# Four GLA heads through one 16-step value product, with merge gates and keys computed beside the GLA levels and kept in DRAM

## The chip, the core and the metric

The kernel runs on one core of one Trainium2 chip. The metric is device time in microseconds of one execution; the time of a kernel is the median of several runs. TensorE (PE) multiplies, VectorE (DVE) and ScalarE (ACT) do the element-wise work, GpSimd (POOL) some of it, and SyncE (SP) issues most DMAs. Each engine works through its own queue in order.

## The reference, cut to what matters

One transformer layer for 256 latent tokens `x` and 256 context tokens `ctx`, width 2048, float32. It has two token mixers side by side (windowed attention A, gated linear attention B), per-channel merge gates, an output projection, and a convolutional FFN.

```python
mod_x = split(silu(c) @ w_mod + b_mod, 6)          # shift, scale, gate twice
qa, ka, va, qb, kb, vb, rb, gf, gb, gate_a, gate_b = project_heads(modulate(x, ...), w_in)
# the same projections of ctx; of them ka, va, kb, vb and the decays are used
o_attn = windowed_attention(qa, ka, va, cka, cva, sink)
sf, sb, _ = context_gla(...)                       # end states of the context
o_gla = latent_gla(qb, kb, vb, gf, gb, sf, sb)     # 4 heads, key width 256, value width 512
y_att = o_attn @ w_attn_o
y_gla = (rms_norm(o_gla, gla_norm) * silu(rb)) @ w_gla_o
x = x + mod_x[2] * ((sigmoid(gate_a) * y_att + sigmoid(gate_b) * y_gla) @ w_out)
x = x + mod_x[5] * conv_ffn(modulate(x, g_ffn, mod_x[3], mod_x[4]), w_up, conv_w, conv_b, w_down)
```

For each GLA head the kernel forms a matrix A (latent rows by latent and context columns, decays included), so that the head's output is A · V with V = h · W_V, h the modulated tokens. By associativity that is also (A · h) · W_V, "the matrix times activations first".

## The kernel before

**Weights.** A float32 product is made of three matmuls on halves. Each 256 x 512 piece of a weight is loaded by SP into a tile `raw` (512 KB; pool `wr`, 7 buffers), rounded by ACT into `whi` (L220), and DVE subtracts to get `wlo` (L221); `whi` and `wlo` have 3 buffers each (`wsplit_raw`). Activations are kept as hi and lo halves too.

**Blocks and ticks.** A block is 512 columns of a weight, contracted in 8 ticks of 256 rows: `proj_nat` (tokens on the output's partitions) and `proj_T` (weight columns on them). With latent and context tokens (`h_xc`, four output tiles, or `h_both`) a tick has 24 matmuls, with latent tokens alone (`h_x`, two tiles) 12. When the block ends, `evac` copies the accumulators out of PSUM. `tick()` and `midway()`, called in each tick, run what was put off to later ticks (`defer`), the next GLA level (`beside`, at a rate per tick), and background steps (`bg_steps` at `bg_rate`): `mod_latent` computes the modulation rows that are needed later from `w_modT`, 96 steps here, each a 512 KB load and one multiply-and-sum on DVE (L403).

**Order.** A scheduler with priorities arranges the instructions on each engine (splits of weights have high priority, and buffers limit how far ahead they can stand); `in_order` pins pairs.

**Stages, in order.** (1) Start, up to 195 us: modulation, the first columns of queries, keys and values of all tokens, group by group; the value columns are head 0's `VB` block, kept in `vb0`. (2) Heads 0 to 3 of GLA, 195 to 435 us: `with_gla(h, kb, block)` runs `gla_A`, the levels that build A of head h, beside a block of projections: `kb_block` (head 0), `v_block` of head 1's values (head 1), `VA` (head 2) and `KA` (head 3), the last two kept in SBUF tiles `va32`, `ka32` (L1060). Heads 0 and 1 multiply A with their values in `gla_o`. (3) The `GA` block for j = 0, and `pair_values` for heads 2 and 3, 435 to 541 us: 8 steps of an `inner` product, 24 matmuls into `pg` (A times 256 columns of h), and an `outer` one, 24 into `acc` (times the weight of two heads). `natural(kp)` normalizes and modulates the 256 columns of x and ctx for a step (L1146, L1152, on DVE and POOL). (4) Attention, 541 to 745. (5) `rb_block`, then the merge: for each j of 0 to 3, 8 ticks each of `GA` (j > 0; L1372 evacuates it), `w_attn_o`, `GB` (L1383 evacuates it, as sigmoid) and `w_gla_o`, up to 1130 us, with the background steps at rate 0.75. (6) `w_out` and the FFN, to the end.

## Time and profile before

| | |
|---|---|
| median of 3 runs | 1946.02 us (1945.85 to 1946.04) |
| the profiled execution | 1945.88 us, its span 1944.1 us |
| PE busy | 1928.8 us (99%), 9906 instructions |
| DVE busy | 1436.2 us (74%) |
| ACT busy | 992.2 us (51%) |
| POOL busy | 58.1 us (3%) |
| DMA | 429.26 MB, 221 GB/s in the mean |
| PE's clock | 1.00 in most windows, 0.999 in the mean |

The span runs from the first to the last instruction. A row of a window lists busy time and instruction counts by engine in this order: PE, PEld (weight load), DVE, ACT, POOL, then PE's granted clock, the share of the DMA engines in use and their rate. In rows of groups, `out<-in xcount | busy, mean ns of one | idle time ahead of it`. In rows of the timeline, the start and the duration come first.

### The profile page before, as it was taken

What the parts mean: (1) busy time and instruction counts of PE and PEld (TensorE: products, weight loads), DVE (VectorE), ACT (ScalarE), POOL (GpSimd) and SP (SyncE); (2) the same over time, 40 slices, a digit from 0 to 9 for tenths busy, and PEclk for the clock granted to TensorE, in tenths of its full rate; (3) what the DMA queues carried; (4) which work ended last, traced back from release to release, by engine and by line L of the source; (5) the groups of instructions that cost most, each with busy time, mean ns of one, the idle gap of its engine ahead of it and who ended that gap; (6) DMA issues with size and microseconds to landing.
All of it is one profiled execution on the core that took longest, in us unless ns stands there. A gap on an engine that the chain in (4) does not pass through costs nothing.

```text
span 1944.1 us, 26485 instructions
## 1 busy us (share of the span) xinstructions
PE 1928.8 (99%) x9906; PEld 1603.9 (83%) x9906; DVE 1436.2 (74%) x2217; ACT 992.2 (51%) x1443; POOL 58.1 (3%) x72
## 2 busy tenths in 40 slices
PE   8999999999999999999999999999999999999999
PEld 6678888888887788888888888888888888888887
DVE  5656867687967889987888577998886545777654
ACT  5223666654456655444444445755565334655532
POOL 0010011020100000000000000000000000000000
PEclk9999999999999999999999999999999999999999
DMA  9984222226554456999999877688886666666663
GB/s 395 412 303 145 67 78 73 78 85 216 179 163 120 141 169 213 350 334 321 334 336 334 300 263 236 200 274 283 274 279 215 193 192 191 187 190 190 195 214 111
DMA packets 188208, 429.26 MB, mean 221 GB/s; under 512 B 12960, under 2 KB 17312, under 8 KB 182832
## 3 DMA queue, kind: packets, MB, share of 16 engines
q1 hardware_dynamic: 186416, 421.84, 65.6%
q0 software_dynamic: 1488, 5.57, 0.9%
q8 instruction: 77, 1.26, 0.3%
q14 instruction: 51, 0.42, 0.1%
q10 hardware_dynamic: 176, 0.17, 0.0%
HBM read 425.37 MB, written 2.16 MB: 220 GB/s over the span
## 4 chain that ended last, share of the span: by engine, by line
PE 96%; DMA 3%; DVE 0%; ACT 0%; issue 0%; SPq 0%
PE acc L84 73%; PE accs L84 13%; PE pa L96 2%; PE pg L84 2%; PE poa L96 1%; PE pS L96 1%; DMA mraw<-in_w_mod 1%; PE pm L96 1%; DMA xr<-in_ctxT 1%; PE ptp L99 1%; DMA raw<-in_w_in 1%; PE po L96 1%; PE pto L99 0%; DMA pack<-in_k_pack 0%; PE plr L646 0%; PE pz L96 0%
## 5 line engine op out<-in xcount | busy, mean ns | idle before, releaser
L220 ACT ACTIVATE whi<-raw 128x1024 fp32r<-128x1024 f32 x568 | 601.2, 1060 | 716.6 <-PE acc L84 541.0
L221 DVE TENSOR_TENSOR wlo<-raw,whi 128x1024 fp32r<-128x1024 f32 x568 | 695.1, 1226 | 348.4 <-ACT whi L220 339.3
L84 PE MATMUL accs<-h,whi 128*128 128x512 f32 x704 | 244.5, 392 | 0.0
L84 PE MATMUL acc<-h,whi 128*128 128x512 f32 x640 | 222.3, 392 | 0.0
L84 PE MATMUL accs<-h,wlo 128*128 128x256 f32 x704 | 196.0, 278 | 0.0
L84 PE MATMUL acc<-h,wlo 128*128 128x256 f32 x640 | 178.1, 278 | 0.0
L84 PEld LDWEIGHTS accs<-h,whi 128*128 128x128 f32 x704 | 131.8, 187 | 29.9
L84 PEld LDWEIGHTS acc<-h,whi 128*128 128x128 f32 x640 | 119.8, 187 | 27.0
L84 PE MATMUL acc<-whi,ah 128*128 128x512 f32 x352 | 137.0, 389 | 0.0
L84 PE MATMUL acc<-whi,al 128*128 128x512 f32 x352 | 137.0, 389 | 0.0
L84 PEld LDWEIGHTS accs<-h,wlo 128*128 128x128 f32 x704 | 132.5, 188 | 0.0
L84 PEld LDWEIGHTS acc<-h,wlo 128*128 128x128 f32 x640 | 120.5, 188 | 0.1
L84 PE MATMUL acc<-whi,h2hi 128*128 128x512 f32 x256 | 101.3, 396 | 0.0
L84 PE MATMUL acc<-whi,th 128*128 128x512 f32 x256 | 100.5, 393 | 0.0
L84 PE MATMUL acc<-whi,h3hi 128*128 128x512 f32 x256 | 100.4, 392 | 0.0
L84 PE MATMUL acc<-whi,h2lo 128*128 128x512 f32 x256 | 99.8, 390 | 0.0
L84 PE MATMUL acc<-whi,h3lo 128*128 128x512 f32 x256 | 99.8, 390 | 0.0
L84 PE MATMUL acc<-whi,tl 128*128 128x512 f32 x256 | 99.7, 389 | 0.0
L84 PE MATMUL acc<-wlo,ah 128*128 128x512 f32 x352 | 94.3, 389 | 0.0
L84 PE MATMUL acc<-whi,h1hi 128*128 128x512 f32 x224 | 88.3, 394 | 0.0
L84 PE MATMUL acc<-whi,h0hi 128*128 128x512 f32 x224 | 87.8, 392 | 0.0
L84 PE MATMUL acc<-whi,h1lo 128*128 128x512 f32 x224 | 87.6, 391 | 0.0
(416 smaller groups left out, 3549.3 us busy)
## 6 DMA issues: line engine op xcount, KB each, us to landing
raw<-in_w_in SPq DMA_DIRECT2D x204, 512.0 KB, 4.3
raw<-in_w_up SPq DMA_DIRECT2D x176, 512.0 KB, 4.4
raw<-in_w_modT SPq DMA_DIRECT2D x128, 512.0 KB, 5.2
raw<-in_w_down SPq DMA_DIRECT2D x88, 512.0 KB, 4.0
mraw<-in_w_mod SPq DMA_DIRECT2D x32, 1024.0 KB, 14.0
raw<-in_w_attn_o SPq DMA_DIRECT2D x32, 512.0 KB, 5.6
raw<-in_w_gla_o SPq DMA_DIRECT2D x32, 512.0 KB, 5.6
raw<-in_w_out SPq DMA_DIRECT2D x32, 512.0 KB, 5.3
```

Of the source, the lines that this page charges most:

```text
L84: r = pe_seq(PE.matmul(*a, **k))
L96: return pe_seq(after(PE.matmul(*a, **k)))
L99: return pe_seq(after(PE.transpose(*a)))
L220: j = S.activation(hi[:, 0:n, :], raw[:, 0:n, :], AF.Copy).ins
L221: i = V.tensor_tensor(lo[:, 0:n, :], raw[:, 0:n, :], hi[:, 0:n, :].bitcast(F32), op=ALU.subtract).ins
```

## The change

1. In stage 1 the values of attention (`VA`, tile `va0`) take the place of head 0's `VB` block; POOL stores them to DRAM (`dva`).
2. All four heads' matrices are kept (`pair_x`, `pair_c`, two pairs); `gla_o` and `v_block` are gone, and `all_values` runs 16 steps of inner and outer products, 8 for each pair.
3. Head 1 has the `KA` block beside it, stored to DRAM (`dka`). Heads 2 and 3 have the four `GA` and the four `GB` blocks beside them (12 matmuls per tick, levels at rate 0.3 per tick). `kept` evacuates two tiles into one buffer of the weight pool and POOL stores it (`da0` to `db3`).
4. Background steps run beside heads 2 and 3 at rate 0.45, and in rb and merge at 0.85. With `share=True`, all of them in the first place and every second one in the other is a multiply on POOL (L415), a sum by ACT (L392) and an addition of one column on DVE. `natural` uses no POOL, and its rows come for two steps at a time.
5. The merge has `w_attn_o` and `w_gla_o` only; POOL fetches the gates from DRAM (`kept_gate`), ACT takes their sigmoid. Keys and values of attention are loaded back from `dka` and `dva` by SP.

The core of the diff:

```diff
-    def mod_latent(parts, begin=None):
+    def mod_latent(parts, begin=None, share=False):
...
+        def drain():
+            while sums:
+                d, c, base = sums.pop(0)
+                in_order(last_lo[0], V.tensor_tensor(d, c, base, op=ALU.add).ins)
+            while open_:
+                raw, d, base, c = open_.pop(0)
+                in_order(last_hi[0], S.activation(raw, raw, AF.Copy, accum_out=c).ins)
+                sums.append((d, c, base))
...
+            drain()
+            if share and (i % 2 == 0 or beside):
+                G.tensor_tensor(raws[i], raws[i], row[0], op=ALU.mult)
+                open_.append((raws[i], d, base, scale1[:, 0, i % 16:i % 16 + 1]))
+                return
             i0 = V.tensor_tensor_reduce(out=raws[i], in0=raws[i], in1=row[0], scale=1.0,
...
-    proj_nat(w_in, 0, VB, kts, h_x, lambda i, b: S.activation(vb0[:, i, :], b, AF.Copy))
+    proj_nat(w_in, 0, VA, kts, h_x, lambda i, b: S.activation(va0[:, i, :], b, AF.Copy))
...
+    dva = dram.tile([P, 4, 512], F32, name="dva")
+    G.dma_start(dva, va0)
...
-    a, kb1 = with_gla(0, kbt, kb_block, [lambda i=i: first_values(i) for i in range(4)])
-    gla_o(0, a, *v)
-    defer(2, send_rows)
-    a, v = with_gla(1, kbt, lambda: v_block(VB + 512, "v1"))
-    gla_o(1, a, *v)
-
-    def kept(c0, name):
-        t = []
+    def kept(c0, name, lhs, by_tile=False):
+        n = len(lhs)
+        d = dram.tile([P, n, 512], F32, name=name)
+        raw = []
 
         def evac(i, b):
-            if not t:
-                t.append(M(name, [P, 4, 512]))
-            S.activation(t[0][:, i, :], b, AF.Copy)
-
-        proj_nat(w_in, 0, c0, ALL, h_xc, evac, by_tile=True)
-        return t[0]
-
-    va32 = with_gla(2, kb1, lambda: kept(VA, "va32"))[1]
+            if i % 2 == 0:
+                raw[:] = [wr.tile([P, 2, 512], F32, name="raw", tag="raw")]
+            S.activation(raw[0][:, i % 2, :], b, AF.Copy)
+            if i % 2:
+                G.dma_start(d[:, i - 1:i + 1, :], raw[0])
+
+        proj_nat(w_in, 0, c0, ALL, lhs, evac, by_tile=by_tile)
+        return d
...
-    ka32 = with_gla(3, kb1, lambda: kept(KA, "ka32"))[1]
+    defer(2, send_rows)
+    kb1 = with_gla(0, kbt, kb_block)
+    dka = with_gla(1, kbt, lambda: kept(KA, "dka", h_xc, True))
+    gate_a, gate_b = [], []
+
+    def gate_blocks(c0, name, to):
+        for j in range(4):
+            if c0 == GB and j == 3:
+                defer(0, lambda: fetch(0))
+                defer(2, lambda: natural(0))
+                defer(5, lambda: natural(1))
+            to.append(kept(c0 + j * 512, f"{name}{j}", h_x))
...
+    bg_rate[:] = [0.45, 0.0]
+    with_gla(2, kb1, lambda: gate_blocks(GA, "da", gate_a), 0.3)
+    with_gla(3, kb1, lambda: gate_blocks(GB, "db", gate_b), 0.3)
+    bg_rate[:] = [0.0, 0.0]
...
-        for kp in range(n + 1):
-            if kp + 1 < n and kp:
-                natural(kp + 1)
-            if kp < n:
-                inner(kp)
-            if kp:
+        for step in range(KT + 1):
+            if 0 < step < KT - 1:
+                natural(step + 1)
+            if step < KT:
+                inner(step)
+            if step:
+                pair, kp = divmod(step - 1, KT // 2)
                 for i in range(2):
                     tick()
...
-    bg_rate[0] = 0.75
+    bg_rate[0] = 0.85
     for j in range(1, 4):
         rb_block(j)
...
+    def kept_gate(d, name):
+        m = [W2("fc", name, [P, 512]) for _ in range(2)]
+        for t in range(2):
+            G.dma_start(m[t], d[:, t, :])
+            i = S.activation(m[t], m[t], AF.Sigmoid)
+            in_order(exps[-1], i.ins)
+            sig.append(i)
+        return m
+
     for j in range(4):
...
+        a1 = kept_gate(gate_a[j], "m1")
+        a2 = kept_gate(gate_b[j], "m2")
...
         proj_nat(A["w_attn_o"][0], 0, j * 512, ALL, [h_tok(1, 0), h_tok(1, 1)], at_evac)
-        proj_nat(w_in, 0, GB + j * 512, ALL, h_x,
-                 lambda t, b, a2=a2: sig.append(S.activation(a2[t], b, AF.Sigmoid)))
```

## The prediction

> **What bounds the kernel now.** I read the page first, then windows by stage, the chain, the waits, and the timeline at block ends.

> ```profile
> span 1944.1 us, 26485 instructions
> PE 1928.8 (99%) x9906; PEld 1603.9 (83%) x9906; DVE 1436.2 (74%) x2217; ACT 992.2 (51%) x1443; POOL 58.1 (3%) x72
> ```

> The profiled execution took 1945.88 us, 0.14 below the median of the three runs (1946.02). TensorE is busy for 99% of it, so only two things can move the time: the number of matmuls, and places at which TensorE would now have to wait. By stage (columns: window, length, busy us of PE, PEld, DVE, ACT, POOL with counts, clock, DMA share, GB/s):

> ```profile
> 0.00:97.00 97.00, 86.69 (x640) 61.03 (x641) 62.68 (x138) 39.63 (x59) 0.84 (x5) 1.00 1.00 404
> 323.50:434.90 111.40, 111.40 (x578) 95.43 (x576) 81.58 (x158) 64.43 (x126) 15.62 (x23) 1.00 0.28 80
> 434.90:541.00 106.10, 106.10 (x477) 87.89 (x476) 85.01 (x126) 46.78 (x66) 13.13 (x9) 1.00 0.61 186
> 745.00:1130.00 385.00, 385.00 (x1734) 318.77 (x1733) 309.35 (x376) 170.50 (x183) 0.00 (x0) 1.00 0.90 317
> 1830.00:1944.10 114.10, 109.53 (x484) 90.35 (x483) 63.70 (x71) 44.03 (x46) 0.00 (x0) 0.99 0.52 167
> ```

> TensorE idles 10.3 us before 97 and 4.6 us after 1830, both outside the change; in the stages that the change rebuilds (323 to 541: heads 2 and 3, the GA block, the paired values; 745 to 1130: rb and merge) it idles for nothing. So no wait can be removed there, only work.

> **What the change removes and adds on TensorE.** Heads 0 and 1 lose their value blocks (192 matmuls of v1; the VB block of head 0 only changes places with VA, whose later block of 192 goes) and two `gla_o` of 24. They gain eight more steps of inner and outer products, 24 + 24 each. 192 + 192 + 48 − 192 − 192 = 48 matmuls fewer. Their price, from the chain:

> ```profile
> 256.32 5.44 PE po L96 x24
> 456.14 10.88 PE pg L84 x48
> 467.02 5.44 PE acc L84 x24
> ```

> 24 take 5.44 us, and the 48 `pg` take 10.88. **Term 1: −10.9 us**, all on the path, since TensorE is the path. The GA and GB blocks only move from the merge to heads 2 and 3, at the same number of matmuls.

> **What stands at a block's end.** TensorE is gapless because the splits of the next block stand ahead of the copies that empty the last one. At the end of a GB block in the merge (ACT, then PE; start, duration):

> ```profile
> 920.55 1.06 ACT L220 ACTIVATE whi<-raw 128x1024 fp32r<-128x1024 f32 x1 [1.66 <-PE acc L84]
> 921.52 1.06 ACT L1383 ACTIVATE m<-acc 128x512 f32<-128x512 f32 x2
> ...
> 920.12 0.39 PE L84 MATMUL acc<-whi,h3lo 128*128 128x512 f32 x1
> 920.35 1.07 PE L84 MATMUL acc<-wlo,h3hi 128*128 128x512 f32 x4
> 921.26 0.39 PE L84 MATMUL acc<-whi,th 128*128 128x512 f32 x1
> ```

> The block's last matmuls end at 921.42 and the next block's first began at 921.26, on a split made beforehand; the two copies followed at 921.52. The order of ACT shows the same, two splits of the next block (`whi_7486`, `whi_7507`) ahead of the copies:

> ```order
> L220 ACTIVATE whi_7486<-raw_7484 128x1024 [waits DMAHW7_49,DVE_49,PE_49]
> L220 ACTIVATE whi_7507<-raw_7505 128x1024 [waits DMAHW1_49,DVE_49,PE_49]
> L1383 ACTIVATE m2_7111<-acc_7295 128x512 [waits PE_49]
> L1383 ACTIVATE m2_7112<-acc_7296 128x512 [waits PE_49]
> L220 ACTIVATE whi_7528<-raw_7526 128x1024 [waits DMAHW3_49,DVE_49,PE_49]
> ```

> After the change, ACT at the end of gate block `da1` in head 2 (`whi_3312` is the first split of `da2`; `raw_3303` holds the two kept tiles; `raw_3219` and `raw_3280` are modulation products of POOL that ACT sums):

> ```order
> L916 ACTIVATE k2_3368<-segs_2619 128x8x32
> L1026 ACTIVATE raw_3303<-acc_3056 128x512 [waits DMASW1_49,PE_49]
> L1026 ACTIVATE raw_3303<-acc_3057 128x512 [waits PE_49]
> L220 ACTIVATE whi_3312<-raw_3310 128x1024 [waits DMAHW6_49,Activation_49]
> L392 ACTIVATE raw_3219,scale1_102<-raw_3219 128x1024 [waits Pool_49]
> L220 ACTIVATE whi_3348<-raw_3346 128x1024 [waits DMAHW0_49,Activation_49]
> ```

> The first split has moved behind both copies, and the copies wait for the block's last matmul: ACT can't prepare the next block, and TensorE has nothing of it to do. The same order stands at eight of the boundaries: from `dka` to `da0`, the three between the GA blocks, `da3` to `db0`, and the three between the GB blocks. At the ninth, `db3` to the value steps, two inner products (24 matmuls each, 10.9 us) stand in between and cover it.

> Price of one, put on the rows above: the second copy starts 0.04 us after the last matmul's shown end (as the split at 920.55 does after 920.12 + 0.39), at 921.46; half of the `x2` row is 0.53, and

> ```profile
> L1383 ACT ACTIVATE m<-acc 128x512 f32<-128x512 f32 x8 | 4.4, 586 | 2.1 <-PE acc L84 2.1
> L220 ACT ACTIVATE whi<-raw 128x1024 fp32r<-128x1024 f32 x568 | 601.2, 1060 | 716.6 <-PE acc L84 541.0
> ```

> with 0.59 it ends at 922.05, the split at 923.11, and TensorE takes it up at about 923.2 where it had been at 921.26: 1.95 us. Least: copy and split alone, 1.65; where k2 exponentials stand ahead too (two of the eight), 2.5. **Term 2: 8 × 1.95 = +15.6 us**, ends 13.2 and 18. The split of wlo (1.23 us) comes while the eight matmuls with whi run (1.8 us), and hides.

> **Stores and the loads behind them.** Each kept pair of tiles sits in a buffer of the weight pool until POOL's store has landed, and the pool's order decides which load waits for it. SP before, in head 3 (L105 carries every load):

> ```order
> L105 DMA raw_3245<-in_w_in 128x2x512 [waits DMAHW5_49,DVE_49,Activation_49]
> L105 DMA raw_3311<-in_w_in 128x2x512 [waits DMAHW6_49,DVE_49]
> L105 DMA raw_3366<-in_w_in 128x2x512 [waits DMAHW7_49,DVE_49,Activation_49]
> L105 DMA raw_3428<-in_w_in 128x2x512 [waits DMAHW0_49,DVE_49,Activation_49]
> L105 DMA raw_3485<-in_w_in 128x2x512 [waits DMAHW1_49,DVE_49,Activation_49]
> ```

> SP after, over gate block `da2` (DMASW4 is the landing of `da1`'s store, `raw_3401` the block's fourth weight piece):

> ```order
> L105 DMA raw_3310<-in_w_in 128x2x512 [waits DMAHW6_49,DMAHW2_49,DVE_49]
> L105 DMA raw_3341<-in_w_modT 128x1024 [waits DMAHW3_49,DVE_49]
> L105 DMA raw_3346<-in_w_in 128x2x512 [waits DMAHW0_49,Activation_49]
> L105 DMA raw_3383<-in_w_in 128x2x512 [waits DMAHW5_49,DMAHW1_49,DVE_49]
> L105 DMA raw_3401<-in_w_in 128x2x512 [waits DMASW4_49,Activation_49]
> L105 DMA raw_3439<-in_w_modT 128x1024 [waits Activation_49]
> L105 DMA raw_3444<-in_w_in 128x2x512 [waits DMAHW6_49,DMAHW4_49,DVE_49]
> ```

> Before, loads waited only for splits; now one waits for a store, with two more loads queued behind it. The nearest rows for the path:

> ```profile
> raw<-in_w_in SPq DMA_DIRECT2D x204, 512.0 KB, 4.3
> att<-in_k_amask POOLq DMA_DIRECT2D x1, 512.0 KB, 4.4
> out<-yd SPq DMA_DIRECT2D x8, 256.0 KB, 4.4
> L1085 POOL DMA_DIRECT2D att<-in_k_amask x1 | 0.5, 536 | 2.6 <-ACT q L921 2.6
> ```

> From the block's end: copies 0.9 us, POOL's issue 0.54 (up to 2.5 more if it stands in a multiply), store 4.4, load 4.3, split 1.06: 11.2 to 13.7 us. The fourth piece is needed three ticks later, 3 × 2.72 = 8.2 us, and the drain of 1.95 and the early first use add some 2: 10.1 to 11. A shortfall of 0 to 2 us, in the five of the eight blocks where the order puts such a load so early. **Term 3: +5 us**, one each; ends 0 and 10.

> **DVE and POOL.** 61 products of the modulation leave DVE (L403) for POOL, ACT sums them (61 × 1.06 more on an engine that is half idle), DVE adds one column. The rows of before show what POOL and DVE do to each other:

> ```profile
> 472.17 1.29 POOL L1152 TENSOR_TENSOR raw<-raw,rows 128x512 f32<-128x512 f32 x1 [7.29 <-DVE raw L1146]
> 472.73 1.80 DVE L221 TENSOR_TENSOR wlo<-raw,whi 128x1024 fp32r<-128x1024 f32 x1 [0.70 <-ACT whi L220]
> 506.91 1.22 DVE L221 TENSOR_TENSOR wlo<-raw,whi 128x1024 fp32r<-128x1024 f32 x1
> 507.14 2.14 POOL L1152 TENSOR_TENSOR raw<-raw,rows 128x512 f32<-128x512 f32 x1 [2.98 <-DVE raw L1146]
> L403 DVE CUSTOM_DVE_ANT_0 raw<-raw,csrow,pack 128x1024 f32<-128x1024 f32 x64 | 81.7, 1279 | 0.0
> L221 DVE TENSOR_TENSOR wlo<-raw,whi 128x1024 fp32r<-128x1024 f32 x568 | 695.1, 1226 | 348.4 <-ACT whi L220 339.3
> ```

> Where they meet, the second one grows by what is left of the first: 472.17 + 1.29 = 473.46, and DVE ends 1.07 after that; 506.91 + 1.22 = 508.13, POOL 1.15 after. They take turns. So a 128x1024 multiply on POOL, twice 1.2 or about 2.45 us by this estimate, is time lost to DVE, where the same product took 1.28 on DVE itself: the move adds load. By budgets: heads 2 and 3 now last 64 ticks × 2.72 = 174.2 plus their own products 24.3 (the 111.4 of the window less 384 matmuls at 0.2268), 198.5 us, 214 with term 2. DVE and POOL together need 64 × 1.2 = 77, the levels about 60 (81.6 in that window, less 15 splits at 1.23 and some small ones), 10 for the two `natural` steps, 27 × 2.45 = 66, and 5 for gates: 218. In rb and merge 88 ticks make 248 us, against 88 × 1.2 + 35 × 1.28 + 34 × 2.45 + 19 = 253; some 20 of it, which read PSUM, may run beside POOL. Both stand at the edge. Where the pair falls behind, wlo is late and TensorE waits; the store of the gates stands behind POOL's multiplies. **Term 4: +4 us**, ends 0 and 25, the low end taken since the rates spread the steps evenly and PSUM work overlaps.

> [...]

> **DMA in the merge.** The merge streamed these bytes:

> ```profile
> 954.00:1042.00 88.00, 88.00 (x394) 72.85 (x393) 72.52 (x90) 37.16 (x39) 0.00 (x0) 1.00 0.95 330
> 49.00:97.00 48.00, 47.20 (x318) 30.39 (x318) 33.32 (x73) 12.87 (x18) 0.00 (x0) 1.00 1.02 413
> ```

> After, a tick of 2.72 us loads 1 + 0.85 pieces of 0.524 MB, 356 GB/s, plus gate reads of 4.2 MB over 248 us, 17: 373 GB/s, under the 413 that the early stage reached. I add nothing, and keep it as a rival. The other additions hide: a step of the values is 10.9 us of matmuls against two splits and a `natural`, 2 × 1.23 + 4 × 0.61 + 2 × 0.69 + 1.23 = 7.5 us on DVE, and some 1 for the halves of `pg`, by these rows:

> ```profile
> L1146 DVE SCALAR_TENSOR_TENSOR raw<-raw,pack,rows 128x256 f32<-128x256 f32 x32 | 18.3, 606 | 0.0
> L1152 DVE TENSOR_TENSOR raw<-raw,rows 128x512 f32<-128x512 f32 x8 | 5.5, 692 | 0.2
> ```

> `dka`, `dva` come back 512 KB at a time ahead of their use; the 16 sigmoids (0.6 us each) stand on ACT at 37 of 88 us.

> [...]

> **Sum.** 1945.9 − 10.9 + 15.6 + 5 + 4 = 1959.6, and with 0.1 to the median 1959.7: 1960 us, 0.7% slower.

> **Rivals.**
> Drains at their least and nothing else: 1946.0 − 10.9 + 13.2 = 1948.3, to about 1949.9; for it, POOL and DVE at the edge but not over, and stores that land before their successor is needed; against it, five loads whose path is longer than their lead.
> The other side, faster: a boundary costs under 10.9 / 8 = 1.36 us, if the first copy runs early (tile 0 is done 0.45 us before tile 1) and level products of head 2 or 3 fill TensorE at the boundary. At 0.8 us each it would be 1946 − 10.9 + 6.4 = 1941.5. Against it: the second copy and the split alone are 1.65 us, and these products wait for exponentials on the same ACT.
> The port: POOL and DVE fall behind in both stages. At 2.6 us a multiply instead of 2.45 and no overlap with PSUM work, 6 + 14 us instead of term 4, about 1975.
> The merge by DMA: in 954 to 1042 a share of 0.95 moved 330 GB/s, so the engines would be full at 347 there; 373 is 7% above that, up to 18 us of 248. Half of it, since rb's ticks and the 413 of the early stage say that the limit lies between: +9 in place of term 4's part, 1964 to 1974.

> **How the numbers follow.** Drains with late loads 0.55 (1950 to 1968); drains at their least 0.12; faster 0.04; the port 0.19 (1968 to 1985); DMA 0.10. The range 1948 to 1977 leaves out the faster case and the upper part of the port's. A measurement of this kernel can tell about 0.2%, 3.9 us, from no change: under 1942.1 is 0.04, to 1949.9 0.13, above 0.83.

> **What would show it.** Eight idle stretches of TensorE near 1.95 us at L1026 block ends, released by ACT whi L220; waits of the fourth weight piece of a gate block; POOL at L415 of 2.4 us or more and wlo far above 1.23 beside it; the merge without idle time. Wrong if TensorE runs through the boundaries, or if wlo rather than whi is what it waits for.

## The result, and the profile after

The changed kernel takes 2052.93 us (median of 4 runs, 2049.63 to 2056.86) against 1946.03: a ratio of 1.055 (95% interval 1.0531 to 1.0568), 107 us slower. The prediction said 1960, with a range to 1977. Of the four runs of e3 below, one took 3225.33 us at a granted clock of 0.556, and all figures of e3 are those of the other three.

Page of the changed kernel (its profiled execution took 2056.86 us):

```profile
span 2055.1 us, 26710 instructions
PE 1957.2 (95%) x9858; PEld 1612.2 (78%) x9858; DVE 1507.6 (73%) x2228; ACT 1066.8 (52%) x1591; POOL 222.5 (11%) x152
...
L221 DVE TENSOR_TENSOR wlo<-raw,whi 128x1024 fp32r<-128x1024 f32 x568 | 713.9, 1262 | 385.2 <-ACT whi L220 379.6
...
L415 POOL TENSOR_TENSOR raw<-raw,csrow 128x1024 f32<-128x1024 f32 x61 | 166.7, 2735 | 466.5 <-DVE qT L63 216.0
```

Two subtractions on the second line give the account. TensorE idles for 2055.1 − 1957.2 = 97.9 us, where it idled for 15.3: **82.6 us of waits**. It is busy for 28.4 us longer although it has 48 matmuls (10.9 us) less: **39.3 us of slower matmuls**. 82.6 + 39.3 − 10.9 = 111.0, the difference of the spans. The clock agrees: it was 0.979 in the mean of this execution, which is 43 us of 2055.1, part of it while TensorE stood still. The windows say where (columns as before: PE, PEld, DVE, ACT, POOL, clock, DMA share, GB/s):

```profile
200.00:313.00 113.00, 111.77 (x577) 94.35 (x574) 86.61 (x169) 73.26 (x148) 15.21 (x18) 1.00 0.23 69
313.00:542.00 229.00, 190.84 (x842) 154.27 (x840) 177.94 (x216) 128.70 (x214) 77.62 (x41) 0.90 0.61 206
542.00:600.00 58.00, 46.53 (x188) 38.07 (x189) 30.35 (x40) 22.22 (x28) 14.45 (x17) 0.83 0.66 220
600.00:920.00 320.00, 317.25 (x1446) 257.81 (x1444) 245.52 (x468) 166.50 (x279) 2.96 (x2) 1.00 0.52 160
920.00:1000.00 80.00, 73.07 (x335) 57.79 (x335) 71.74 (x113) 48.74 (x81) 17.10 (x7) 0.98 0.65 217
1000.00:1200.00 200.00, 177.18 (x756) 141.65 (x755) 164.22 (x169) 103.79 (x138) 78.15 (x40) 0.96 0.87 303
```

Beside the gate blocks (313 to 542) TensorE idles for 38 us, in the last gate block (542 to 585; the first value steps behind it, to 600, run without a wait) for 11, in the end of attention and rb (920 to 1000) for 7, in the merge (1000 to 1200) for 23. In the same windows, and only there, the clock column falls below 1.00. What ended the waits from 313 to 545 (us in total, times, longest):

```profile
PE acc L84 <- ACT whi L220: 22.8, 8, 9.5
PE acc L84 <- DVE wlo L221: 17.9, 6, 4.2
```

The eight on `whi` are the eight boundaries: seven drains of 1.63 to 2.76 us, 13.3 in all, and the one of 9.5 us, which has a late load in it. Six of the seven blocks that open with a short drain have a wait on `wlo` 3 to 7 us later; the prediction's sum had no such wait. Timeline at the boundary from `da0` to `da1`, PE, DVE and POOL:

```profile
341.74 0.50 PE L84 MATMUL acc<-whi,h0hi 128*128 128x512 f32 x1 [1.82 <-ACT whi L220]
...
343.43 0.63 PE L84 MATMUL acc<-whi,h0hi 128*128 128x512 f32 x1
343.85 0.63 PE L84 MATMUL acc<-whi,h0lo 128*128 128x512 f32 x1
348.63 1.65 PE L84 MATMUL acc<-wlo,h0hi 128*128 128x512 f32 x3 [4.15 <-DVE wlo L221]
...
340.80 2.88 DVE L917 TENSOR_TENSOR k<-k,kb 128x512 f32<-128x512 f32 x1
343.61 2.57 DVE L920 TENSOR_TENSOR segs<-segs 128x256 f32<-128x256 f32 x1
...
347.38 3.47 DVE L221 TENSOR_TENSOR wlo<-raw,whi 128x1024 fp32r<-128x1024 f32 x3
...
339.99 0.60 POOL L1028 DMA_DIRECT2D da<-raw  x1 [8.47 <-ACT raw L1026]
340.61 5.29 POOL L415 TENSOR_TENSOR raw<-raw,csrow 128x1024 f32<-128x1024 f32 x2
```

The drain is 1.82 us, close to the price of 1.95. POOL had stood for 8.47 us at the store of the kept tiles, which waits for ACT's copies at the block's end; two multiplies behind it in POOL's queue start back to back as soon as the store is issued, 5.29 us, in the very moment in which DVE has to make the next `wlo`. DVE's `k` product, 0.68 us elsewhere, takes 2.88, and the next small one, 0.42 elsewhere, takes 2.57: each ends just after a multiply of POOL has ended. They stand ahead of `wlo` in DVE's queue, and TensorE waits 4.15 us for it. From 343.00 on matmuls start 0.42 to 0.43 us apart instead of 0.23. The other boundaries look alike: where two multiplies start behind the store (340.61, 406.37, 467.23, 502.23) the wait for `wlo` is 3.7 to 4.2 us, where one does (376.40, 440.51) 0.7 and 1.4.

At the end of the gates, SP's queue and then PE:

```profile
516.34 0.37 SPq L105 DMA_DIRECT2D raw<-in_w_in  x1
532.44 0.34 SPq L105 DMA_DIRECT2D rows<-drows  x1
...
535.11 0.44 SPq L105 DMA_DIRECT2D raw<-in_w_in  x1
...
544.51 0.80 PE L84 MATMUL acc<-whi,h0hi 128*128 128x512 f32 x1 [9.45 <-ACT whi L220]
```

SP stands for 16 us ahead of a load of normalization rows, whose memory belongs to head 3's levels until ACT's L936 has read it; five other transfers come out behind it within 3 us, too late for the start of the last gate block. From 535.6 SP then stands for another 16 us, until the store of block `db2` has landed. POOL issued that store only at 548.66, behind its fetches and products for the attention; TensorE waits 7.16 us at 558.94, still in the last gate block. In the merge, ACT and then PE:

```profile
1084.40 0.63 ACT L1364 ACTIVATE m<-m 128x512 f32<-128x512 f32 x1 [9.06 <-DMA m<-db]
1084.93 1.04 ACT L220 ACTIVATE whi<-raw 128x1024 fp32r<-128x1024 f32 x1
...
1086.03 0.79 PE L84 MATMUL acc<-whi,h2hi 128*128 128x512 f32 x1 [5.03 <-ACT whi L220]
```

ACT stands for 9 us in a sigmoid that waits for the fetch of its gate, with a split behind it for which TensorE waits 5 us.

### The profile page after: what moved, and what is told of

The parts are those of the page before. It is cut to its first block, busy times and chain, and to the rows that moved or that the text cites. A ratio compares the mean times of both kernels' runs of the same rounds, so it can differ in the third digit from the quotient of the medians.

```text
span 2055.1 us, 26710 instructions
## 1 busy us (share of the span) xinstructions
PE 1957.2 (95%) x9858; PEld 1612.2 (78%) x9858; DVE 1507.6 (73%) x2228; ACT 1066.8 (52%) x1591; POOL 222.5 (11%) x152
## 4 chain that ended last, share of the span: by engine, by line
PE 58%; DMA 7%; DVE 6%; ACT 2%; issue 2%; POOL 1%; SPq 0%; ACTq 0%; DVEq 0%; POOLq 0%
PE acc L84 40%; PE accs L84 12%; DMA raw<-in_w_in 3%; DVE wlo L221 3%; PE pg L84 2%; ACT whi L220 1%; DMA raw<-in_w_modT 1%; PE pS L96 1%; PE poa L96 1%; DMA m<-db 1%; DMA raw<-in_w_attn_o 1%; POOL raw L415 1%; PE ptp L99 1%; DMA m<-da 1%; DMA raw<-in_w_gla_o 0%
## 5 line engine op out<-in xcount | busy, mean ns | idle before, releaser
L221 DVE TENSOR_TENSOR wlo<-raw,whi 128x1024 fp32r<-128x1024 f32 x568 | 713.9, 1262 | 385.2 <-ACT whi L220 379.6
L220 ACT ACTIVATE whi<-raw 128x1024 fp32r<-128x1024 f32 x568 | 599.9, 1060 | 681.1 <-PE acc L84 358.2
L84 PE MATMUL accs<-h,whi 128*128 128x512 f32 x704 | 244.5, 392 | 0.0
L84 PE MATMUL acc<-h,whi 128*128 128x512 f32 x640 | 222.3, 392 | 0.0
L415 POOL TENSOR_TENSOR raw<-raw,csrow 128x1024 f32<-128x1024 f32 x61 | 166.7, 2735 | 466.5 <-DVE qT L63 216.0
L84 PE MATMUL accs<-h,wlo 128*128 128x256 f32 x704 | 196.0, 278 | 0.0
L84 PE MATMUL acc<-h,wlo 128*128 128x256 f32 x640 | 178.1, 278 | 0.0
L84 PEld LDWEIGHTS accs<-h,whi 128*128 128x128 f32 x704 | 131.8, 187 | 29.8
L84 PEld LDWEIGHTS acc<-h,whi 128*128 128x128 f32 x640 | 119.8, 187 | 27.0
L84 PE MATMUL acc<-whi,ah 128*128 128x512 f32 x352 | 137.1, 389 | 0.0
L84 PE MATMUL acc<-whi,al 128*128 128x512 f32 x352 | 137.0, 389 | 0.0
L84 PEld LDWEIGHTS accs<-h,wlo 128*128 128x128 f32 x704 | 132.6, 188 | 0.0
L84 PEld LDWEIGHTS acc<-h,wlo 128*128 128x128 f32 x640 | 120.5, 188 | 0.1
L84 PE MATMUL acc<-whi,h3hi 128*128 128x512 f32 x256 | 102.4, 400 | 5.1 <-ACT whi L220 5.1
L84 PE MATMUL acc<-whi,h2hi 128*128 128x512 f32 x256 | 102.4, 400 | 5.0 <-ACT whi L220 5.0
L84 PE MATMUL acc<-whi,h0hi 128*128 128x512 f32 x192 | 82.3, 429 | 23.5 <-ACT whi L220 23.5
L84 PE MATMUL acc<-whi,th 128*128 128x512 f32 x256 | 101.1, 395 | 3.0 <-ACT whi L220 3.0
L84 PE MATMUL acc<-whi,h3lo 128*128 128x512 f32 x256 | 101.3, 396 | 0.0
L84 PE MATMUL acc<-whi,h2lo 128*128 128x512 f32 x256 | 100.9, 394 | 0.0
L84 PE MATMUL acc<-whi,tl 128*128 128x512 f32 x256 | 100.2, 391 | 0.0
L84 PE MATMUL acc<-wlo,ah 128*128 128x512 f32 x352 | 94.2, 389 | 0.0
L84 PE MATMUL acc<-whi,h1hi 128*128 128x512 f32 x192 | 77.4, 403 | 13.7 <-ACT whi L220 13.7
## 6 DMA issues: line engine op xcount, KB each, us to landing
raw<-in_w_in SPq DMA_DIRECT2D x204, 512.0 KB, 4.4
raw<-in_w_up SPq DMA_DIRECT2D x176, 512.0 KB, 4.3
raw<-in_w_modT SPq DMA_DIRECT2D x128, 512.0 KB, 5.0
raw<-in_w_down SPq DMA_DIRECT2D x88, 512.0 KB, 3.8
raw<-in_w_attn_o SPq DMA_DIRECT2D x32, 512.0 KB, 6.1
raw<-in_w_gla_o SPq DMA_DIRECT2D x32, 512.0 KB, 5.8
raw<-in_w_out SPq DMA_DIRECT2D x32, 512.0 KB, 6.0
```

Source lines behind the costliest of these rows:

```text
L84: r = pe_seq(PE.matmul(*a, **k))
L220: j = S.activation(hi[:, 0:n, :], raw[:, 0:n, :], AF.Copy).ins
L221: i = V.tensor_tensor(lo[:, 0:n, :], raw[:, 0:n, :], hi[:, 0:n, :].bitcast(F32), op=ALU.subtract).ins
L415: G.tensor_tensor(raws[i], raws[i], row[0], op=ALU.mult)
```

## The experiments

The theories: **drain** (the order of copies and splits), **port** (POOL's multiplies hold DVE up), **clock** (a wait is followed by matmuls at half rate), **queue** (loads behind a waiting load), **gate fetch** (ACT in a sigmoid), **DMA** (too many bytes in the merge). Times are medians; 1946.0 to 1946.4 for the kernel before beside them.

### e1: the port, taken away

```diff
-    bg_steps.extend(mod_latent(((3, shift2), (4, scale2), (2, gcol1)), share=True))
+    bg_steps.extend(mod_latent(((3, shift2), (4, scale2), (2, gcol1))))
```

> The changed kernel with share=False: all modulation products on DVE in one instruction (1.28 us), none on POOL, no sums on ACT. Theory port: POOL's multiplies lock DVE out, so wlo is late; in the profile of the changed kernel TensorE waits for wlo at six places beside the gates, 19.8 us, and 24 us in the merge, plus the half-clock matmuls behind those waits. It expects these six to go, and about half of the merge's: 2053 - 20 - 12 - 10 (clock) = some 2010 us. Rival drain: wlo is late only because the block's restart finds DVE's queue full behind the drained boundary; then the six stay within a few us and the time stays above 2040. Rival DVE-bound: DVE's own load of 1.28 instead of 0.15 us a step makes it slower than 2053.

1989.77 us (ratio 1.0224, 1.0208 to 1.0239): 63 us off, where 43 were expected. PE's waits from 313 to 545:

```profile
PE acc L84 <- ACT whi L220: 24.0, 10, 7.0
PE acc L84 <- DVE wlo L221: 0.4, 1, 0.4
```

The waits for `wlo` are gone and those for `whi` have stayed: POOL's multiplies make `wlo` late, with the drains in place. The edit takes ACT's 61 sums away too, and no run takes those away alone; since the waits for `whi`, which ACT makes, did not shrink here, and e8 below has such sums and no wait for `whi`, they are the less likely cause. DVE, given back 61 products of 1.28 us, is busy for less time than before (1468.1 us instead of 1507.6): the time in which DVE's instructions stood waiting for POOL had counted as busy, like the 2.88 us of the `k` product above.

### e2 and e3: the drains, taken away

```diff
+        def later_evac(i, b):
+            done.append((i, b))
+            if i == n - 1:
+                defer(1, lambda: [evac(*a) for a in done])
```

used by all gate blocks but the last, in e2 alone and in e3 with the edit of e1.

> The changed kernel with the copies of each gate block put off to the second tick of the next block, so that its first split stands ahead of them (not at the last of the eight boundaries' predecessor dka to da0, which stays). Theory drain: seven of eight drains go, 7 x 1.95 = 13.7 us, and the half-clock stretches that follow them, some 5: about 2034 us, and the wlo waits go too if the drained restart causes them: about 2010. Theory port: the drains go, the wlo waits stay: 2034 to 2040. The waits at db3 and the first value steps (19 us) stay by both.

> Both edits of the two kernels before it. If drains and the port are two causes that add, the gain is the sum of both, about 50 to 60 us, some 1995 us; what is left above 1935 (before less 10.9) is loads that stand behind waiting instructions at db3 and the values, and the gates' fetches in the merge. If one of them is the cause of the other, it gains no more than the better of the two.

e2: 2024.28 us (1.0401, 1.0386 to 1.0417), 29 off. e3: 1971.0 (1.0133, 1.0116 to 1.0149; 1970.65 to 1974.46), 82 off, more than expected. The two edits alone add to 92, so some 10 us are shared. In e2 waits for `wlo` are 9.7 us instead of 17.9 from 313 to 545: some of the port's harm there comes with the drained restart, but more than half of these waits stay without a drain. In e3 none are left there.

### e4 and e10: the price of a drain, and of a longer one

The kernel before, with seven drains in its merge (e4), and the same with the last copy repeated five times (e10):

```diff
+    def drained(t, i):
+        if t:
+            hold_hi.append(i.ins)      # the next block's first whi is pinned behind it
+        return i
```

> The kernel before, in whose merge the first split of the next block is pinned behind the two sigmoid copies at seven block ends (GA of j = 1 to 3, GB of j = 0 to 3): seven drains and nothing else of the change. By the prediction's price 7 x 1.95 = +13.7 us: 1959.7. Theory clock: TensorE runs at half rate for some 2 to 5 us once it has idled, as the changed kernel's rows show after its waits (matmuls at 0.43 instead of 0.23 us): another 1 to 1.8 us each, 1967 to 1972. If a drain is hidden by other work, 1946.

> The kernel before with the seven drains of e4 made longer: the last sigmoid copy is repeated five times (the same data), so that ACT holds the next split back by another 5 x 0.5 to 0.6 us. Idle of TensorE per drain by that: 1.8 + 2.5 to 3.0 = 4.3 to 4.8 us. If an idle stretch costs its own length (as e4's 1.83 us cost 2.0), 7 x 4.5 = +31: 1976 to 1981. Theory clock: after a longer idle stretch matmuls run at half rate for some us, which costs 1.2 to 2.4 us each in the changed kernel's rows: +9 to +17 on top, 1986 to 1996.

e4: 1960.24 us, +14.0, 2.0 for each drain. e10: 1996.61, +50.6, 7.2 for each. PE after the first drain, e4:

```profile
835.45 0.50 PE L84 MATMUL acc<-whi,th 128*128 128x512 f32 x1 [1.67 <-ACT whi L220]
835.79 0.40 PE L84 MATMUL acc<-whi,tl 128*128 128x512 f32 x1
836.03 0.40 PE L84 MATMUL acc<-whi,th 128*128 128x512 f32 x1
```

and e10:

```profile
838.33 0.80 PE L84 MATMUL acc<-whi,th 128*128 128x512 f32 x1 [4.81 <-ACT whi L220]
838.92 0.63 PE L84 MATMUL acc<-whi,tl 128*128 128x512 f32 x1
839.35 0.63 PE L84 MATMUL acc<-whi,th 128*128 128x512 f32 x1
...
841.91 1.73 PE L84 MATMUL acc<-wlo,th 128*128 128x512 f32 x4
843.48 0.39 PE L84 MATMUL acc<-whi,th 128*128 128x512 f32 x1
```

After 1.67 us of idling (the longest of e4's seven waits; 11.7 in all) matmuls go on at a pitch of 0.24 us. After 4.81 us they go at 0.43 for some 5 us, and then at 0.23 again: some 2 us more. Both theories of the sizes hold: a short drain costs what the prediction said, and the clock adds to a longer one.

The length alone does not decide, though. In the changed kernel no slow matmul stands between the drains of 1.63, 1.67 and 1.67 us (315.32, 406.45, 440.59) and the next wait, but slow ones follow those of 1.82, 2.76, 1.82 and 1.94 (341.74, 376.49, 468.40, 502.31). And at the boundary from `da1` to `da2`, e3 (first) and e5 have the same wait:

```profile
370.00 0.50 PE L84 MATMUL acc<-whi,h0hi 128*128 128x512 f32 x1 [2.73 <-ACT whi L220]
```

```profile
370.32 0.50 PE L84 MATMUL acc<-whi,h0hi 128*128 128x512 f32 x1 [2.73 <-ACT whi L220]
...
371.61 0.63 PE L84 MATMUL acc<-whi,h0hi 128*128 128x512 f32 x1
```

The granted clock from 363 to 377 is 1.00 in e3 and 0.88 in e5, so the same 2.73 us can cost more or not. The changed kernel's record of the clock says more. Four windows around the drain that ends at 341.74, and two around the one that ends at 440.59 (columns as before):

```profile
339.57:342.98 3.41, 1.59 (x9) 1.20 (x8) 2.96 (x3) 3.09 (x6) 2.97 (x2) 1.00 0.81 316
342.98:346.39 3.41, 1.50 (x4) 0.66 (x2) 3.41 (x3) 1.64 (x3) 2.83 (x2) 0.50 0.27 59
346.39:349.81 3.42, 1.18 (x3) 0.99 (x4) 3.42 (x6) 1.06 (x1) 0.00 (x0) 0.50 0.34 116
349.81:353.22 3.41, 3.41 (x10) 2.64 (x9) 2.24 (x3) 0.00 (x0) 0.00 (x0) 0.50 1.00 291
...
438.55:441.97 3.42, 1.75 (x8) 1.16 (x7) 1.40 (x1) 3.42 (x6) 2.06 (x2) 1.00 0.27 113
441.97:445.38 3.41, 2.03 (x10) 1.35 (x9) 3.41 (x4) 2.54 (x4) 0.96 (x1) 1.00 0.52 154
```

In this trace half rate comes, from 342.98 to 1196.3, in 13 pieces of 3.41 us or two or three times that, whose starts lie whole multiples of 3.41 us apart: a fixed grid. Of the stretches of this grid that ran at full rate, here and in the kernel before, those in which TensorE stood still for 0.57 of the time or more (1.9 us) were always followed by half rate (12 of 12), those with 0.50 or less (1.7 us) never (none of 1121), those between sometimes (3 of 6). Two longer waits of the merge fall across a boundary of the grid, 1131.46 and 1134.88, and matmuls go on at full rate behind both, 0.23 us apart behind the second:

```profile
1131.76 1.20 PE L84 MATMUL acc<-wlo,h1hi 128*128 128x512 f32 x4 [2.10 <-DVE wlo L221]
...
1136.70 0.50 PE L84 MATMUL acc<-whi,h1hi 128*128 128x512 f32 x1 [3.31 <-ACT whi L220]
1137.04 0.39 PE L84 MATMUL acc<-whi,h1lo 128*128 128x512 f32 x1
1137.27 0.39 PE L84 MATMUL acc<-whi,h1hi 128*128 128x512 f32 x1
```

So a wait was cheap here if it was short, or if the grid cut it in two. That this also tells e3's 2.73 us from e5's is an estimate from these rows.

### e5 and e6: a queue and the gates' fetches

e3 with, in e5, loads of rows pinned behind the load before them and POOL's fetches for attention behind the last gate store; in e6, the sigmoids put off and pinned behind the last split made by then:

```diff
+            before = last_load[0]
+            in_order(before, load(r, drows[kp:kp + 2]...))
...
+        defer(at, sigmoids)            # at = 6 ticks for m1, 12 for m2
```

> The kernel of e3 with two pins on queues: the load of the normalization rows for steps 2 and 3 of the values no longer stands in SP's queue ahead of older loads (it waits there for the GLA levels to give up its memory, in the changed kernel from 516 to 532 us with five loads behind it), and POOL's fetches of the attention mask, rope and norms stand behind the last gate store. Theory queue: the waits at the end of the gates and the first value steps (1.6 and 4.2 us in e3, half-clock matmuls behind them) go: 5 to 9 us below e3's 1972.7. Rival: these loads are late because of the stores' landings themselves; then nothing changes beyond 2 us.

> The kernel of e3 with the sigmoids of the fetched gates put off by 6 ticks (first gate) and 12 ticks (second), behind the splits made by then. Theory gate fetch: in the merge ACT stands in a sigmoid that waits for its fetch, with splits queued behind it; about 8 of the 11 us of waits in the merge go, and half-clock matmuls behind them: 1960 to 1965. Rival DMA: the merge is short of loads (0.94 of the DMA engines' time at 340 GB/s, whi waiting for loads of w_gla_o and w_attn_o 60 us in total), and the splits are late whatever ACT does: within 4 us of 1972.7.

e5: 1969.69 us, 1.3 off e3 where 5 to 9 were expected, and no more than e3's own spread. The two waits of 1.5 and 4.0 us go, and one of 2.1 comes up 10 us later, at a load that waits for the last but one store. So these two pins are not shown to gain anything by themselves. e6: 1960.21, 11 off e3. PE's waits in the merge (1000 to 1200) of e3 and of e6:

```profile
PE acc L84 <- ACT whi L220: 9.4, 7, 2.4
```

```profile
PE acc L84 <- ACT whi L220: 0.8, 2, 0.6
```

The sigmoids were the merge's wait, once POOL's multiplies were gone.

### e8: the port alone, in a gapless stage

The kernel before with `share=True`: 48 of its modulation steps on POOL, in rb and the merge but for four, which POOL takes up earlier, beside the attention.

> The kernel before, in which every second modulation step in rb and the merge (48 of them) is a multiply on POOL, a sum on ACT and a small addition on DVE, at the old rate of 0.75; nothing else of the change. Theory port: each POOL multiply of 2.4 us or more locks DVE out where the step took 1.28 us on DVE before; wlo comes late now and then, and TensorE waits: +5 to +20 us. Rival: in a stage with gapless TensorE and splits made three ahead the 3.4 us that DVE can be late hide it: within 4 us of 1946; then the port only hurts where the queues are already drained.

1962.2 us (1.0083, 1.007 to 1.0097), +15.9, 0.33 for each multiply in the mean. Two windows of e8, the attention and what follows it, and groups of the second:

```profile
541.00:745.00 204.00, 198.81 (x920) 158.65 (x919) 159.23 (x336) 120.27 (x219) 9.94 (x4) 0.99 0.44 140
745.00:1150.00 405.00, 400.57 (x1787) 327.95 (x1785) 353.50 (x347) 224.73 (x286) 134.11 (x45) 1.00 0.89 309
```

```profile
L221 DVE TENSOR_TENSOR wlo<-raw,whi 128x1024 fp32r<-128x1024 f32 x141 | 177.8, 1270 | 49.6 <-ACT whi L220 48.9
...
L415 POOL TENSOR_TENSOR raw<-raw,csrow 128x1024 f32<-128x1024 f32 x44 | 133.6, 3036 | 225.6 <-DMA raw<-in_w_modT 133.7 <-DVE wlo L221 35.3 <-DMA csrow<-csd 13.6
...
L418 DVE CUSTOM_DVE_ANT_0 raw<-raw,csrow,pack 128x1024 f32<-128x1024 f32 x22 | 53.9, 2449 | 0.0
```

A multiply takes 3.04 us on POOL, and the 22 products of this form that stayed on DVE take 2.45 us instead of 1.28 (the other 24 there 2.9 to 3.4). Sharing costs 16 us without a single drain, but not evenly: TensorE idles for 5.2 us in the attention, beside four multiplies (0.3 in the kernel before), and for 4.4 in rb and the merge, beside 44 (none before). All waits behind this idling are for DVE: 4.8 us in the first window, for the softmax, and 4.2 in the second, 2.6 of them for `wlo`.

### e7, e11, e12, e13: what put the splits behind the copies

e7 is e3 with e5 and e6, and background steps also beside the values (0.45 per tick there, 0.7 in the merge). e11 is the changed kernel with this edit alone, e12 is e7 with it in place of the late copies, e13 is e12 with the changed kernel's rates:

```diff
-                raw[:] = [wr.tile([P, 2, 512], F32, name="raw", tag="raw")]
+                if not ring or used[0] == 2:
+                    ring[:], used[0] = [M("keep", [P, 2, 2, 512])], 0
+                raw[:] = [ring[0][:, used[0]]]
+                used[0] += 1
```

> e3 with the edits of e5 and e6, and background steps also beside the values (rate 0.45), so that the merge needs 0.7 per tick instead of 0.85 (about 330 instead of 373 GB/s asked of the DMA). If drains, port, queues, gate fetches and the merge's DMA are all that the change lost, what is left is the 48 matmuls, less a last drain from dka to da0: 1946 - 10.9 + 2 + some 3 = about 1940, faster than before. If something else is open, it stays above 1946.

> The changed kernel with one edit: kept blocks are copied to a buffer of their own instead of one of the weight pool's seven, all else (POOL's share, the order of the code) as it is. The order of ACT then has one split of the next block ahead of the copies at nearly every boundary again. Theory pool: the shared pool is what put the splits behind the copies and made loads wait for stores; the drains (16 us) and their half-clock stretches go, and the late load at db3 in part: 2015 to 2025, as e2 or better. Rival: the scheduler's order is not what cost; above 2040. The wlo waits of the port theory stay (20 us).

> e7 with the copies at the block's end again, but into a buffer of their own. e7 was left with 10.7 us of waits: 1.2 in head 0, 1.8 behind dka, 2.9 and 1.1 for loads held by the stores, 3.7 at the first value steps for a load held by a store, and their half-clock matmuls. If the shared pool caused the last four, 7 to 10 us go: 1940 to 1943, 0.15 to 0.3% faster than before. If they are of another cause, 1948 to 1950.

> e12 with the changed kernel's rates: no background steps beside the values, 0.85 per tick in rb and the merge (some 370 GB/s asked of the DMA there, against 340 with 0.7). Theory DMA: the merge is short of loads at that rate: 5 to 9 us slower than e12. Rival: with the sigmoids out of ACT's way the loads hide: within 2 us of e12.

e7: 1949.72 us (1.0012, 1.0003 to 1.0021), where some 1940 were expected. e11: 2012.23 (1.0338, 1.0324 to 1.0353), 41 off, more than e2. PE's waits of e11 from 313 to 545:

```profile
PE acc L84 <- DVE wlo L221: 7.9, 7, 2.0
PE acc L84 <- ACT whi L220: 5.4, 2, 4.2
```

ACT at the end of `da1` in e11:

```profile
366.82 1.05 ACT L220 ACTIVATE whi<-raw 128x1024 fp32r<-128x1024 f32 x1
367.77 1.06 ACT L1031 ACTIVATE keep<-acc 128x512 f32<-128x512 f32 x2
```

With a buffer of its own for the kept tiles, the scheduler puts a split ahead of the copies again, with no pin: taking the buffer from the weight pool had set the order. The same edit gives the pool its buffers back and keeps loads from waiting for stores, so its 41 us are not those of the order alone. In e12 (1949.08; 1.0015, 1.0006 to 1.0024) no boundary is left, but the time is that of e7, so the shared pool was not what e7 still lost: a wait of 1.8 us for `whi` is left, and one of 6.6 us at the second inner product, for halves of `pg` that ACT takes up behind a split whose weight is 6.1 us late. e13: 1950.83 (1.0023, 1.0014 to 1.0032). The intervals overlap: what the rate in the merge costs is some 4 us at most, and these runs do not tell it from nothing.

### e14 and e15: is the saving there?

e14 is e12 with the loads for the first normalization one block earlier, the normalization at ticks 0 and 4 instead of 2 and 5, no background steps beside it, and the rates raised elsewhere to make up for it. e15 goes back to ticks 2 and 5 and keeps the steps away from the keys too. The first lines below are in both, the last two in e15 alone.

```diff
+            if c0 == GB and j == 2:
+                defer(4, lambda: fetch(0))
+            if c0 == GB and j == 3:
+                bg_rate[:] = [0.0, 0.0]
...
+    defer(3, lambda: bg_rate.__setitem__(0, 0.8))
+    defer(13, lambda: bg_rate.__setitem__(0, 0.0))
```

> e12 with the first normalization of the values one block earlier (its rows and x loaded in the third GB block, natural(0) and natural(1) at ticks 0 and 4 of the last), and no background steps in the last GB block and the first steps of the values (0.5 after that, 0.72 in rb and the merge). In e12 two waits are left, 1.9 and 6.8 us at the first value steps, where h's halves for step 1 come late, and 2.6 us of half-clock matmuls behind them. If with those the loss is complete, the 48 matmuls that the change saves show: 1949 - 11 = 1936 to 1940, 0.3 to 0.5% faster than before. If the saving is not there, it stays at 1946 or above.

> e14 with its last waits addressed by moving work on DVE only: no background steps while the keys are normalized (0.8 per tick in ticks 3 to 12 of the values, none after; 0.77 in rb and the merge), and natural(0) at tick 2 instead of 0 of the last GB block. e14's profile has 6 us of waits left: 2.9 at the last products of head 3's levels, behind natural(0), and 3.7 at the keys. If DVE's load there causes them, 4 to 6 us go: 1937 to 1940. If they have another cause, 1942 to 1945.

e14: 1943.82 us (0.9988, 0.9979 to 0.9997), where 1936 to 1940 were expected. e15: 1940.06 (0.9967, 0.9955 to 0.998), 0.3% faster than the kernel before. Its page, and its windows from the gates to the merge:

```profile
span 1937.2 us, 26517 instructions
PE 1919.4 (99%) x9858; PEld 1595.4 (82%) x9858; DVE 1466.0 (76%) x2289; ACT 1004.0 (52%) x1469; POOL 54.7 (3%) x91
```

```profile
313.00:500.00 187.00, 187.00 (x911) 158.06 (x910) 160.97 (x250) 109.85 (x173) 11.54 (x15) 1.00 0.80 261
500.00:720.00 220.00, 218.12 (x969) 179.41 (x968) 168.79 (x263) 101.82 (x150) 9.17 (x18) 1.00 0.66 218
720.00:915.00 195.00, 194.81 (x926) 156.55 (x925) 168.65 (x360) 116.52 (x207) 1.07 (x2) 1.00 0.50 160
915.00:1140.00 225.00, 225.00 (x1018) 186.11 (x1017) 186.21 (x231) 105.35 (x118) 9.63 (x18) 1.00 0.95 346
```

Against before, TensorE is busy for 9.4 us less and idles for 2.5 more. So the 48 matmuls are worth nearly their price, and the loss had no other large part: with the products on DVE, the kept tiles in a buffer of their own, and sigmoids, rows and background steps at other places, the heads beside the gates and the merge run without a gap. How the last few us divide among these moves no run shows.

## Why the prediction was wrong, step by step

**Term 1 (−10.9), right.** 9.4 us less of busy time in e15, 10.9 by the matmuls' price.

**Term 2 (+15.6, 1.95 each), right in place and size.** All eight boundaries wait; the seven not mixed with a late load take 1.6 to 2.8 us, 1.9 in the mean, and e4 gives 2.0 for each. What four of the seven brought behind them, matmuls at half rate, was not in the price. That the order had changed was read from the order; its cause, the shared pool, was not looked for.

**Term 3 (+5 for late loads), the wrong place.** Loads were followed that wait for a store, up to block `da2`. What came out is further on: a load of rows that waits for memory of head 3's levels, with five transfers behind it, and a store that stands in POOL's queue behind the attention's fetches. They gave waits of 9.5 and 7.2 us, both in the last gate block, not 1 us at each of five.

**Term 4 (+4 for the port), the step that failed most.** Two pairs of rows of before (a split of 1.80 us beside a multiply instead of 1.23, a multiply of 2.14 us beside a split instead of 1.29) were read as POOL and DVE taking turns, and the budgets came out at 100%; then the low end was taken because the rates spread the steps evenly and work on PSUM runs beside POOL. The second holds for a pair of before: a copy from PSUM (L873) takes 0.46 us at 357.71, beside a product of POOL (357.70, 0.75 us), and 0.45 elsewhere. The first does not: the gate's store stands ahead of multiplies in POOL's queue and holds them until the block's end, so they start, two at a time at four boundaries, just when DVE restarts. The prediction had this the other way round, with the store behind the multiplies. (No run moves the stores off POOL's queue; this part is read from the timeline.) A multiply takes 2.7 us in the mean (3.0 in e8) instead of 2.45, and what costs is less its length than the small DVE instructions ahead of `wlo`, which end only with a multiply (2.88 us instead of 0.68, 2.57 instead of 0.42); most `wlo`, by the prediction's sign far above 1.23 us, take 1.22 as before (from 313 to 542 the median is 1.22, the mean 1.43, one 5.74). With the multiplies taken away the kernel is 63 us faster (e1). The rival "the port" expected a late `wlo`, by budgets that run over, at a price of 20 us.

**Missing: the clock.** 39 us of the loss, by the subtraction above, are slower matmuls, and the rows show them at half rate behind waits. The granted clock of before is 1.00 nearly everywhere, so no row of it showed the price; e10 shows it, 2 us on top of a wait of 5. Part of e1's 63 us is this clock, which rose from 0.979 to 0.993.

**Missing: the gate fetch.** The sixteen sigmoids were costed as 0.6 us each on an idle ACT; what is behind them in ACT's queue while their fetch is late was not asked. It is worth 11 us with the multiplies and most drains gone (e6). "The merge without idle time", a sign of the prediction, did not come: TensorE idles there for 23 us.

**The DMA rival** can't be told from nothing once the sigmoids are out of ACT's way (e13). With e15 the merge runs at 346 GB/s and a DMA share of 0.95 without idle time.

## What to carry to other kernels

Where the bounding engine has no gap, a change that saves work on it is decided by the order at the seams: a buffer taken from the pool that feeds it can turn that order (41 us between the changed kernel and e11, with the late loads), and an instruction that waits for a transfer costs what stands behind it in its queue (9.06 us of a sigmoid, 5.03 us of TensorE behind it). A budget near 100% on POOL and DVE, which lengthen each other's instructions (a product on DVE 2.45 us instead of 1.28 in e8), was no slack here but a loss, and more of one where short instructions of the late engine stand ahead of what is waited for (63 us by e1, the clock's part in it). A store that waits for a block's end holds everything behind it in its queue back until that moment (8.47 us on POOL at 339.99). A wait of TensorE cost more than its length where the granted clock fell behind it: where it filled more than about half of a stretch of 3.41 us, and not after waits of 1.67 us and less.
